# The end of a streaming top-10 kernel: its last three tiles scheduled by hand, with finer exponentials, split gathers, and one batch's rows on the scalar engine

## Chip, cores and metric

One core of one Trainium2 chip. The metric is the device time of one execution in microseconds (us); lower is better. The kernel before took 683.44 us (median of 3 runs, 682.90 to 683.74).

The rounds of the experiments ran on three chips, always with the kernel before beside them, so runs of different rounds are compared by their ratio to it. A time is about 1.8 us more than the span of the profile of the same run.

## The reference

```python
def setup_inputs():
    return {"x": np.random.randn(8192, 8192).astype(np.float32), "k": 10}

def reference(x, k):
    indices = np.argpartition(x, -k, axis=1)[:, -k:]
    values = np.take_along_axis(x, indices, axis=1)
    sorted_idx = np.argsort(-values, axis=1)
    return np.take_along_axis(indices, sorted_idx, axis=1)
```

For each of 8192 rows: the positions of the ten largest of 8192 numbers, largest first. x is 268 MB, and every byte of it must be read once.

## The kernel before

The rows go through in 64 tiles of 128 rows (4 MB). A row is folded over several partitions, and in each tile this happens:

1. *load*: four or eight transfers on the SyncE queue bring in the tile; four x buffers.
2. *weigh*: ACT computes exp(36 (x - 4.7)) into a bf16 tile `e`, and PE adds up groups of columns of it with one-hot matrices. A group that holds one of the top ten has a large sum.
3. *choose*: DVE finds the 12 largest sums (two searches of eight, with a replacement between) and makes indices of them.
4. *gather*: GpSimd copies the candidates of the chosen groups.
5. *spread* and *extract*: a multiplication by a mask, half on DVE and half on GpSimd, and 12 fp32 matmuls (24 passes on PE) bring each row's candidates together.
6. *rank*, three tiles later: DVE takes the top ten of 96 or 192 candidates.
7. *finish*, once per batch of eight tiles or fewer: positions are turned into column numbers (slot, low, two products over a one-hot tile, a sum, the value), spread out as `rows`, moved across partitions by PE ("moves"), copied and written out.

The last three tiles, 61, 62 and 63, use a thin layout (16 partitions to a row, 2 KB pieces). The last batches are of 7, 6 and 3 tiles. At the very end a check counts that all went well, and otherwise a slow loop does the work again. The parts that the change touches:

```python
PAD = 208                       # a spacer tile of 208 floats, allocated ahead of the x buffers
...
    epool = ctx.enter_context(tc.tile_pool(name="e", bufs=3))
...
    nsums = 2 * ntiles + 3      # one checked sum per activation; the size of eall and good
...
    def weigh(t):
        ...
        parts = [S // 4, S // 4, S // 4, S // 8, S // 8] if t == last else [S // 2, S // 2]
        for h, n in enumerate(parts):
            e = epool.tile([P, N // 2], bf16, tag="e", name="e")
            nc.scalar.activation(out=e[:, 0:n * W], in_=xts[t][...], func=ACTF.Exp, ...)
            ...                                   # the sums of this part, on PE
...
        for t in range(last):                     # every engine keeps this order
            interleave(choose_steps(t), rank_steps(t - LAG) if t >= LAG else [])
            if t >= 1:
                spread(t - 1)
            gather(t)
            weigh(t + 1)
            if 1 <= t < last - 2:
                extract(t - 1)
            ...                                   # some finish steps of an earlier batch
        extract(last - 3)
        extract(last - 2)
        run(choose_steps(last))
        spread(last - 1)
        gather(last)
        extract(last - 1)
        ...
        run(rank_steps(last - 3))
        run(rank_steps(last - 2))
        steps = finish_steps(batch_of[last - 3])  # the batch of six
        run(steps[:2])
        spread(last, G)
        run(steps[2:7])                           # ends with its rows, on DVE
        extract(last)
        run(steps[7:-2])                          # its six moves
        run(rank_steps(last - 1))
        run(rank_steps(last))
        ...
        final = finish_steps(batch_of[last])
```

## Time and profile before

| before | us |
|---|---|
| time, median of 3 runs | 683.44 |
| span of the trace | 679.8 |
| last byte of x lands | 651.40 |
| DVE's first search in tile 62's sums | 647.00 |
| DVE's first search in the last tile's sums | 653.96 |
| last ranking ends | 672.88 |

The prediction below shows the page's slices, the windows of the tail and the tail's timeline, and reads them. Of the timeline of the kernel before, the columns are start, duration, engine, line, operation, output and inputs, and in brackets how long the engine had been idle and what ended that.

```profile
647.00 0.70 DVE L189 MAX8 wall<-s 128x8 f32<-128x512 f32 x1 [4.73 <-PE s L169]
675.33 0.62 PE L281 MATMUL fo<-rows,send 128*48 128x80 f32 x6 [1.11 <-DVE rows L301]
```

DVE was idle for 4.73 us before the sums of tile 62 came, and for 1.61 us before those of the last tile. The first is room for other work of DVE. The second is slack on the path: tile 62's sums could come 1.61 us later before the last search moved. PE had slack too, for it waited 1.91 us for ACT before tile 62's sums.

### The profile page before, as it was taken

The page shows a single profiled execution, that of the slowest core. Times are in us where ns is not written, and L with a number is a line of the kernel's source. Part 1 is how long each engine was busy: PE and PEld are TensorE (multiplying, and loading weights), DVE is VectorE, ACT ScalarE, POOL GpSimd, SP SyncE. Part 2 cuts the span into 40 slices and gives each one's busy share as a digit, 9 for nine tenths or more (in the row PEclk, how much of TensorE's full clock was granted, in tenths as well). Part 3 has the DMA queues.
Part 4 walks back from the last instruction along what each step waited for, and adds up shares of the span by engine and source line. Part 5 has one row for each costly group of instructions (what it writes and reads, how often), then busy time and mean ns, then how long its engine had stood idle before and what let it go on. Part 6 is the DMA issues. An engine that isn't in the chain of part 4 may idle for free.

```text
span 679.8 us, 7988 instructions
## 1 busy us (share of the span) xinstructions
PE 549.6 (81%) x2690; PEld 339.5 (50%) x2690; DVE 555.5 (82%) x1335; ACT 488.7 (72%) x264; POOL 178.9 (26%) x134
## 2 busy tenths in 40 slices
PE   1577777888887889887987898898888789887887
PEld 0144544554544565553753555655454355454566
DVE  2577878699779978789796998879977889879687
ACT  4777777777777777777777777777777777777740
POOL 0113133313322322313322313322332231331330
PEclk9887887687878768597686768767788768778786
DMA  9999999999999999999999999999999999999910
GB/s 351 420 421 420 422 418 419 421 419 421 420 420 420 421 419 420 421 419 421 420 421 419 421 419 422 418 420 421 419 421 419 421 419 419 420 420 392 385 39 7
DMA packets 73696, 269.77 MB, mean 397 GB/s; under 512 B 4382, under 2 KB 5046, under 8 KB 73654
## 3 DMA queue, kind: packets, MB, share of 16 engines
q1 hardware_dynamic: 72960, 268.54, 96.8%
q10 hardware_dynamic: 694, 0.71, 0.3%
q8 instruction: 21, 0.34, 0.2%
q14 instruction: 21, 0.17, 0.1%
HBM read 268.58 MB, written 0.66 MB: 396 GB/s over the span
## 4 chain that ended last, share of the span: by engine, by line
DMA 62%; PE 10%; DVE 8%; SPq 6%; ACT 5%; issue 4%; POOL 3%; ACTq 0%; DVEq 0%
DMA xt<-in_x_dram 62%; PE s L169 8%; SPq L101 6%; ACT e L162 5%; POOL cand L203 3%; PE g L233 2%; DVE wall L189 2%; DVE m L190 1%; DVE masked L221 1%; DVE cidb L194 0%; DVE cidb L192 0%; DVE wall L193 0%; DVE rows L301 0%; DVE g L246 0%; DVE pick L298 0%
## 5 line engine op out<-in xcount | busy, mean ns | idle before, releaser
L162 ACT ACTIVATE e<-xt,bias 128x4096 bf16<-128x4096 f32 (+2 forms) x131 | 475.5, 3630 | 155.4 <-DMA xt<-in_x_dram 143.2
L169 PE MATMUL s<-e,group 128*128 128x512 bf16 x1024 | 337.5, 491 | 123.7 <-ACT e L162 123.4
L169 PEld LDWEIGHTS <-group 128*128 128x128 bf16 x1024 | 121.7, 122 | 316.3 <-issue 259.4
L233 PEld LDWEIGHTS g<-cpack,masked 128*128 128x128 f32 x1536 | 206.4, 214 | 16.5 <-issue 5.4
L233 PE MATMUL g<-cpack,masked 128*128 128x8 f32 (+1 forms) x1536 | 199.1, 269 | 1.7 <-DVE masked L221 1.7
L203 POOL INDIRECT_COPY cand<-xt,idx 128x192 f32 x64 | 64.9, 1014 | 478.8 <-DMA xt<-in_x_dram 181.8
L189 DVE MAX8 wall<-s 128x8 f32<-128x1024 f32 (+1 forms) x64 | 77.2, 1206 | 116.2 <-PE s L169 116.1
L221 POOL TENSOR_TENSOR masked<-cand,cpack 128x768 f32<-128x768 f32 x63 | 113.1, 1795 | 5.3
L192 DVE FIND_INDEX8 cidb<-wall,s 128x8 uint16<-128x1024 f32 (+1 forms) x64 | 76.6, 1197 | 0.0
L194 DVE FIND_INDEX8 cidb<-wall,m 128x8 uint16<-128x1024 f32 (+1 forms) x64 | 76.3, 1193 | 0.0
L190 DVE MATCH_REPLACE8 m<-wall,s 128x1024 f32<-128x1024 f32 (+1 forms) x64 | 76.0, 1188 | 0.0
L193 DVE MAX8 wall<-m 128x8 f32<-128x1024 f32 (+1 forms) x64 | 75.6, 1181 | 0.0
L221 DVE TENSOR_TENSOR masked<-cand,cpack 128x768 f32<-128x768 f32 x64 | 61.4, 960 | 0.9 <-POOL cand L203 0.9
L281 PE MATMUL fo<-rows,send 128*64 128x160 f32 (+3 forms) x128 | 27.9, 369 | 1.1 <-DVE rows L301 1.1
L162 ACT ACTIVATION_READ_ACCUMULATOR e<-xt,bias 128x1 f32 x131 | 24.4, 186 | 0.0
L281 PEld LDWEIGHTS fo<-rows,send 128*64 128x64 f32 (+2 forms) x128 | 18.3, 159 | 3.5 <-DVE rows L301 1.6
L248 DVE FIND_INDEX8 posb<-t8a,g 128x8 uint16<-128x96 f32 (+1 forms) x64 | 16.6, 260 | 0.0
L250 DVE FIND_INDEX8 posb<-t8b,g 128x8 uint16<-128x96 f32 (+1 forms) x64 | 16.4, 255 | 0.0
L245 DVE MAX8 t8a<-g 128x8 f32<-128x96 f32 (+1 forms) x64 | 16.1, 252 | 0.0
L246 DVE MATCH_REPLACE8 g<-t8a,g 128x96 f32<-128x96 f32 (+1 forms) x64 | 16.1, 251 | 0.0
L249 DVE MAX8 t8b<-g 128x8 f32<-128x96 f32 (+1 forms) x64 | 15.8, 246 | 0.0
L362 ACT ACTIVATE e<-tall,bias 128x64 f32<-128x64 f32 x1 | 0.3, 347 | 19.6 <-DVE tall L251 19.6
(37 smaller groups left out, 105.7 us busy)
## 6 DMA issues: line engine op xcount, KB each, us to landing
xt<-in_x_dram SPq DMA_DIRECT2D x248, 1024.0 KB, 16.3
xt<-in_x_dram SPq DMA_DIRECT2D x16, 512.0 KB, 9.4
out_dram<-opack ACTq DMA_DIRECT2D x6, 80.0 KB, 5.2
cpack<-topk_cpack ACTq DMA_DIRECT2D x1, 141.0 KB, 3.3
out_dram<-opack ACTq DMA_DIRECT2D x1, 70.0 KB
out_dram<-opack SPq DMA_DIRECT2D x1, 60.0 KB, 1.9
out_dram<-opack SPq DMA_DIRECT2D x1, 30.0 KB, 1.5
```

The source lines that it names most:

```text
L101: nc.sync.dma_start(out=dst[:, s:s + n, :], in_=src[:, s:s + n, :])
L162: nc.scalar.activation(out=e[:, 0:n * W], in_=xts[t][:, s0 * W:(s0 + n) * W], func=ACTF.Exp, bias=bias[:, 0:1], scale=BETA, accum_out=eall ...
L169: nc.tensor.matmul(ss[t][:, j:j + BANK], lhsT=lay.group[:, s0 + i, :], rhs=e[:, i * W + j:i * W + j + BANK], start=s0 + i == 0, stop=s0 + ...
L189: lambda: nc.vector.max(out=w16[:, 0:8], in_=m),
L190: lambda: nc.vector.match_replace(out=m2, in_to_replace=w16[:, 0:8], in_values=m, imm_value=-1.0),
L192: lambda: nc.vector.max_index(out=cid[:, 0:8], in_max=w16[:, 0:8], in_values=m),
L193: lambda: nc.vector.max(out=w16[:, 8:16], in_=m2),
L194: lambda: nc.vector.max_index(out=cid[:, 8:16], in_max=w16[:, 8:16], in_values=m2),
L203: nc.gpsimd.add_instruction(mybir.InstIndirectCopy(name=nc.get_next_instruction_name(), ins=[nc.gpsimd.lower_ap(xts[t]), nc.gpsimd.lower_a ...
L221: eng.tensor_tensor(out=masked[t][:, g0:g1], in0=cand[:, g0:g1].unsqueeze(2).to_broadcast(shape), in1=layout(t).own.rearrange("p (c s) -> ...
L233: nc.tensor.matmul(gs[t][:, c * R:(c + 1) * R], lhsT=mk[:, c, :, :].rearrange("p a s -> p (a s)"), rhs=layout(t).place, start=True, stop=True)
L281: nc.tensor.matmul(fo, lhsT=lay.send[:, i, 0:n * S], rhs=rows[:, i].rearrange("p a k -> p (a k)"), start=i == 0, stop=i == n - 1)
```

## The change

Its intent: take work out of the 28 us after the last byte of x. It moves the extraction and ranking of tile 60, and four finish steps of the batch of six, ahead of the last tile's sums; cuts the last tiles' exponentials into smaller parts so that PE can put extractions between the sums; gathers the candidates of the last two tiles in two halves, so that masks start sooner; and gives `rows` of the batch of six to ACT, which is idle by then. The core of the diff (cut; the main loop's order of the index search and the replacement is swapped too):

```diff
-PAD = 208
+PAD = 320
...
+    def parts(t):
+        S = layout(t).S
+        if t < ntiles - TAIL:
+            return [S // 2] * 2
+        return [S // 4] + [S // 8] * 5 + [S // 16] * 2 if t == last else [S // 4] * 4
...
-    nsums = 2 * ntiles + 3
+    first_sum = np.cumsum([0] + [len(parts(t)) for t in range(ntiles)]).tolist()
+    nsums = first_sum[-1]
...
+        early = t >= last - 1
         return [
             lambda: nc.vector.max(out=w16[:, 0:8], in_=m),
+            lambda: nc.vector.max_index(out=cid[:, 0:8], in_max=w16[:, 0:8], in_values=m),
+        ] + ([lambda: index(0, G // 2), lambda: gather(t, 0, G // 2)] if early else []) + [
             lambda: nc.vector.match_replace(out=m2, ...),
-            lambda: nc.vector.max_index(out=cid[:, 0:8], in_max=w16[:, 0:8], in_values=m),
             ...
+        def spread_rows():
+            if b != len(starts) - 2:
+                return nc.vector.tensor_tensor(out=rows, ..., op=ALU.mult)
+            for a in range(A):
+                nc.scalar.activation(out=rows[:, :, a, :], in_=val, func=ACTF.Copy,
+                                     scale=lay.own_a[:, a:a + 1])
...
-        extract(last - 3)
-        extract(last - 2)
-        run(choose_steps(last))
-        ...                                       # the old tail, shown above
+        a, b, c = last - 2, last - 1, last        # tiles 61, 62, 63
+        run(later)
+        wb, wc = weigh_steps(b), weigh_steps(c)
+        run(wb[0:3])
+        extract(a - 1, 0, 6)
+        run(wb[3:4])
+        extract(a - 1, 6, G)
+        run(wc[0:4])
+        run(rank_steps(a - 2))
+        mask(nc.gpsimd, a, G // 2, G)
+        run(choose_steps(b))
+        mask(nc.vector, a, 0, G // 2)
+        extract(a, 0, 2)
+        run(wc[4:5])
+        extract(a, 2, 4)
+        run(wc[5:])
+        extract(a, 4, G)
+        run(rank_steps(a - 1))
+        steps = finish_steps(batch_of[a - 1])
+        run(steps[:4])
+        mask(nc.gpsimd, b, G // 2, G)
+        chosen = choose_steps(c)
+        run(chosen[:4])
+        mask(nc.vector, b, 0, G // 2)
+        run(chosen[4:])
+        extract(b)
+        run(steps[4:7])
+        mask(nc.vector, c, 0, G // 2)
+        extract(c, 0, G // 2)
+        ...
+        run(rank_steps(a))
+        mask(nc.vector, c, G // 2, G)
+        extract(c, G // 2, G)
+        run(steps[7:])
+        run(rank_steps(b))
+        run(rank_steps(c))
```

## The prediction

> **What bounds the kernel now.** I read the page first, from the slices down to the chain, then two stretches of the end in the table of windows, then the timeline of the last 40 us line by line.
>
> ```profile
> span 679.8 us, 7988 instructions
> PE   1577777888887889887987898898888789887887
> DVE  2577878699779978789796998879977889879687
> ACT  4777777777777777777777777777777777777740
> DMA  9999999999999999999999999999999999999910
> GB/s 351 420 421 420 422 418 419 421 419 421 420 420 420 421 419 420 421 419 421 420 421 419 421 419 422 418 420 421 419 421 419 421 419 419 420 420 392 385 39 7
> ...
> DMA 62%; PE 10%; DVE 8%; SPq 6%; ACT 5%; issue 4%; POOL 3%; ACTq 0%; DVEq 0%
> ```
>
> The DMA row stands at 9 in 38 of 40 slices and the rate is flat at 420 GB/s: until about 651 us nothing but the arrival of x sets the time, and PE, DVE and ACT all have idle time. The last two slices are different: DMA and ACT are done, PE and DVE are not. The last three tiles use the thin layout (2 KB rows), and the rate in their slices is 392 and 385. By the landing times in the trace the last 4 MB tile arrives in eight pieces from 642.4 to 651.4 us, 1.29 us apart. So 679.8 - 651.4 = 28 us of tail after the last byte is all that this change can touch; the 651 us before it stay.
>
> ```profile
> core 0: us, PE busy (x) PEld busy (x) DVE busy (x) ACT busy (x) POOL busy (x), PEclk, DMA share, GB/s
> 653.90:672.90 19.00, 19.00 (x105) 18.51 (x104) 17.55 (x56) 0.00 (x0) 3.54 (x3) 0.59 0.00 1
> 672.90:679.80 6.90, 2.13 (x13) 1.17 (x11) 3.31 (x12) 0.35 (x1) 0.00 (x0) 0.75 0.05 15
> ```
>
> The tail has two parts. From the last tile's sum (653.9) to the end of its ranking (672.9), DVE is busy 17.55 of 19.0 us and PE all of it: both are bounds, and a change must relieve both. ACT has nothing to do there. From 672.9 on comes a serial end of 6.9 us (last batch's rows, the move, the check, the branch).
>
> ```profile
> 651.40 0.95 DVE L221 TENSOR_TENSOR masked<-cand,cpack 128x768 f32<-128x768 f32 x1
> 652.05 1.13 ACT L162 ACTIVATE e<-xt,bias 128x1024 bf16<-128x1024 f32 x1
> 653.54 17.21 PEld L233 LDWEIGHTS g<-cpack,masked 128*128 128x128 f32 x96
> 653.96 0.70 DVE L189 MAX8 wall<-s 128x8 f32<-128x512 f32 x1 [1.61 <-PE s L169]
> 658.30 0.94 DVE L221 TENSOR_TENSOR masked<-cand,cpack 128x768 f32<-128x768 f32 x1
> 663.66 1.76 DVE L221 TENSOR_TENSOR masked<-cand,cpack 128x1536 f32<-128x1536 f32 x1 [0.88 <-POOL cand L203]
> 668.03 1.16 DVE L301 TENSOR_TENSOR rows<-val,cpack 128x960 f32<-128x960 f32 x1
> 672.75 0.14 DVE L251 COPY tall<-t8b 128x1 f32<-128x1 f32 x1
> 677.16 0.15 DVE L377 CAST ngood<-gps 1x1 int32<-1x1 f32 x1 [0.37 <-PE gps L375]
> ```
>
> The third line is four extractions (tiles 60 to 63, 24 passes each) in one lump after the last sum, although the masks of tile 60 were ready 18 us earlier. The other lines mark DVE's way through the tail; its only real waits there are 1.61 us on the last sum and 0.88 us on the gather of tile 63.
>
> **What the Trainium skill says.** "TensorE: Matmul & The Clock Gate", Part 1: the array's clock is half until the monitor has seen a busy window of about 3.4 us, and falls back after an idle one. The trace agrees on the two values and the 3.4 us grid, but not on what counts as busy: from 657.5 us the clock is 0.5 for 17 us although the extractions run back to back. One pass takes 110 ns before and 214 ns after that, so 24 passes are 2.65 or 5.1 us. I expect half clock again once the 512-wide sums end.
>
> "ScalarE: Activation LUTs", What ACT_TABLE_LOAD costs: an activation with a [128,1] pointer operand takes about 280 ns + 0.833 ns per element, overlapping its neighbour by 93 ns. The trace agrees: 2048 columns take 1.98 us, and starts are 1.99 apart. Table sets: copy is in every set, so the new copies should need no second table load; no run here shows that yet.
>
> "SBUF — State Buffer", Who interferes with whom: a DVE instruction with two SBUF inputs contends with a GpSimd one that reads SBUF. GpSimd's mask takes 1.80 us beside a busy DVE and 1.54 late in the tail, so this is a few tenths, off the path.
>
> **The change part by part.** Durations are start-to-start distances in the timeline of before: choosing a thin tile 4.34 us (653.96 to 658.30), ranking 1.34 (96 columns) or 1.86 (192), half a mask 0.94, slot and low 0.27, the two products over the one-hot tile 0.93 and 0.57, their sum and the value 0.93 and 0.26, rows 1.07.
>
> *Exponentials.* ACT takes 1.99, 1.13 and, extrapolated, 0.68 us for 2048, 1024 and 512 columns. Tile 61 and 62 go from two to four activations, the last from five (2048 x3, 1024 x2) to eight (2048, 1024 x5, 512 x2). That is about 0.25 us more per extra one, some 1.8 us in all, against pieces that can start earlier. But only three e buffers remain, so each activation now waits for the sums three parts back. In tile 61 the fourth waits: PE is in the moves of an earlier batch until 632.85, so I put its start at about 634 in place of 630.75. In the last tile the fourth and eighth wait behind extractions in PE's order. Following ACT and PE part by part I get the last sum at 653.4 if no buffer binds and 654.5 if they do, against 653.96. No gain from this part; its use is to have sums of tile 62 out near 646.1 (before: 647.0).
>
> *Extractions between sums.* Tile 60's extraction and a third of tile 61's go before the last sum. After it PE has 16 + 24 + 24 passes in place of 96. At half clock the 32 removed are 6.9 us, but PE is only one of two bounds.
>
> *DVE between last sum and last ranking.* Before: 18.91 us. Moved ahead of the last sum: tile 60's ranking (1.34) and four steps of the six-tile batch (0.27 + 0.93 + 0.57 = 1.77). Moved to ACT: rows (1.07). The wait for the gather (0.88) goes, since half the candidates are gathered early and other work lies in the way. Added: one more index instruction, 0.3, and a split mask, 0.15. 18.91 - 1.34 - 1.77 - 1.07 - 0.88 + 0.45 = 14.3 us. Moved work must fit before the last sum: from tile 62's sum at 646.1, choose 4.2 (with the extra index), mask 0.94, rank 1.34, four steps 1.77 make 654.3. So DVE arrives just as the last sum does; I take 654.3 as the start.
>
> *Does PE follow?* The last half mask of tile 63 ends 14.3 - 1.86 - 1.86 = 10.6 us after the start, at 664.9; its 12 passes at half clock take 2.6, plus 0.2 to be seen, 667.7; DVE has ranked tile 62 by 666.7. So DVE waits 0.9 us. Last ranking ends 654.3 + 14.3 + 0.9 = 669.5 (before 672.87).
>
> *ACT's rows.* 16 copies of 60 columns. An estimate from the skill's figures: 280 + 50 - 93 = 237 ns each, 3.8 us, from about 661 to 665, under the extractions. Then 12 move passes on PE after the last extraction, 3.44 us at half clock (670.79 in before), end near 671, when the last batch needs PE at about 672. Just hidden.
>
> *The end.* The last batch's steps are the same: 6.93 us. 669.5 + 6.93 = 676.4, that is 3.4 us under 679.8. Median: 683.44 - 3.4 = 680.0. Splitting the last loads and the wider check cost nothing on this path. I choose 679.7, a little lower, because the buffer waits are the term I took most harshly.
>
> **The rivals.** (1) PE stays the bound: everything after 657 at half clock, moves and extractions queue, and the last batch's move waits for the other batch's twelve passes. For it: half clock for 17 us in before. Against: 32 passes fewer. Gain 1.5 us or less: 681.9 or more. (2) ACT becomes the bound at the end of the stream, through the added fixed cost and the three buffers; the last sum comes at 655.5 or later, and everything after shifts by that. For it: in before ACT runs without a gap from 641.2 to 653.2. Against: pieces arrive 1.29 us apart and 1024 columns need 1.13. It would make about 681.5. (3) All waits vanish: the sum at 653.4, PE at full clock, the rankings back to back: 653.4 + 14.3 + 6.9 = 674.6, a time of 678.2. (4) The shifted buffer addresses (x moves by 512 bytes) or the swapped order of the index search and the replacement in the main loop change the stream itself. The DMA rate is flat at 420 GB/s whatever DVE does, so I expect nothing; were it 1%, that would be 7 us either way.
>
> **Range and chances.** The sum gives 680.0; rivals 1 to 3 span 678.2 to 682. Range 677.2 to 682.0. 2% is 13.7 us, half of the tail, more than removing all of DVE's moved work could give; so faster by 2% has 1%, slower 1% (only through rival 4), within 2% 98%.
>
> **What would show it.** Right: the chain is DMA until 651, the last sum near 654.3, DVE without a long gap from 646 to 669, the last ranking near 669.5, 16 short activations under the extractions, a last part of 6.9 us. Wrong: a gap over 1.5 us ahead of the last ranking with PE named (rival 1); ACT activations late behind PE releases and the last sum past 655 (rival 2); another DMA rate in the middle slices (rival 4); or a second table load.

## The result, and the profile after

The changed kernel took 682.18 us (median of four runs: 680.32, 681.59, 682.78, 683.04), beside 683.28 for the kernel before in the same rounds. The ratio is 0.998, with a 95% interval of 0.9957 to 1.0003: the same time. A ratio here is the mean time of one kernel's fast runs over the mean of the other's in the same rounds, so it is not quite the ratio of the two medians. The class was predicted; the time was not. 682.18 lies 0.2 us above the range, and 2.5 above the predicted time.

The stations of the tail, each read from the timelines:

| us | predicted | before | after |
|---|---|---|---|
| DVE's first search in tile 62's sums | 646.1 | 647.00 | 649.40 |
| DVE's first search in the last tile's sums | 654.3 | 653.96 | 658.11 |
| from there to the end of the last ranking | 15.2 | 18.92 | 15.41 |
| from there to the end of the span | 6.93 | 6.94 | 7.44 |
| span | 676.4 | 679.8 | 681.0 |

So the tail after the last sums did become 3.5 us shorter, nearly as predicted. But the last sums are searched 4.15 us later, although the last byte of x lands at the same time (651.40 before, 651.45 after). The gain was given away ahead of the stretch that was tuned.

From the page of the changed kernel, the rate of each slice, and the shares of the chain that ended last:

```profile
GB/s 360 420 422 420 420 420 418 421 419 421 419 421 420 419 420 420 421 418 422 420 421 419 421 419 421 419 420 421 419 422 419 420 419 421 418 419 382 370 29 7
...
PE 5%; DVE 1%; issue 0%; ACT 0%; DVEq 0%
```

The middle slices still move 420 GB/s, so the stream itself is as before. The chain has changed: before, it came back to the DMA of x for 62% of the span; now no transfer of x is in it at all. It breaks off before it gets to one. What is in it, in order of time (start, duration, what):

```profile
642.96 4.29 PE s L183 x12
647.25 1.24 PE g L264 x12
648.49 0.89 PE s L183 x4
```

PE's own queue leads to DVE's search at 649.40: twelve sums of tile 62, then the first twelve passes of the extraction of tile 60 (L264), then the last four sums of tile 62. The timeline shows the rest of the story:

```profile
637.21 2.00 ACT L176 ACTIVATE e<-xt,bias 128x2048 bf16<-128x2048 f32 x1 [6.90 <-PE s L183]
649.40 0.70 DVE L217 MAX8 wall<-s 128x8 f32<-128x512 f32 x1 [2.28 <-PE s L183]
650.94 0.86 DVE L209 TENSOR_SCALAR idx<-cidb,cpack 128x6 uint16<-128x6 uint16 x1
658.11 0.70 DVE L217 MAX8 wall<-s 128x8 f32<-128x512 f32 x1
664.36 3.88 ACT L319 ACTIVATE rows<-val,cpack 128x60 f32<-128x60 f32 x16 [7.18 <-DVE val L348]
671.58 0.37 DVE L277 MAX8 t8a<-g 128x8 f32<-128x192 f32 x1 [1.67 <-PE g L264]
676.04 1.03 PE L330 MATMUL fo<-rows,send 128*48 128x80 f32 x6 [1.14 <-DVE rows L314]
```

The line at 658.11 has no bracket: DVE did not wait for the last sums. It ran from 649.40 to 658.11 without a gap, through its choice in tile 62, a mask, the ranking of tile 60 and four finish steps, and only then could it turn to the last tile. The search in the last tile is no longer tied to the arrival of x. It is tied to tile 62's sums, 8.71 us ahead of it. The first line is an exponential of tile 61, the last of its four parts. It waited 6.90 us for an `e` buffer, which PE had not yet read.

The same in windows: first the approach to tile 62's sums, before and then after, and then after's tail. The columns are named in the first line of the second fence.

```profile
631.90:649.40 17.50, 13.92 (x66) 7.23 (x65) 11.22 (x39) 14.64 (x11) 6.87 (x5) 0.85 0.89 339
```

```profile
core 0: us, PE busy (x) PEld busy (x) DVE busy (x) ACT busy (x) POOL busy (x), PEclk, DMA share, GB/s
631.90:649.40 17.50, 17.00 (x86) 10.81 (x86) 10.24 (x38) 12.19 (x13) 3.31 (x4) 0.78 0.90 339
658.10:673.50 15.40, 15.40 (x72) 14.92 (x72) 13.31 (x44) 3.88 (x16) 3.03 (x3) 0.50 0.00 1
```

In this window of 17.5 us, which ends where after's tile 62 is searched, PE went from 13.9 us of work to 17.0: it is full. A part of the rise is the lower clock (0.78 in place of 0.85). The work that was moved out of the tail sits in PE's queue in front of the sums that the tail now starts from.

The theories that I then had:

- **A, the buffer wait.** Rival 2 of the prediction: the 6.90 us wait of ACT for an `e` buffer delays every part after it. Without the wait the sums come as predicted.
- **B, DVE's chain behind PE's queue.** The end is tile 62's first search plus 8.7 plus 15.3 plus 7.3 us, whatever ACT does, and tile 62's search is set by the work in PE's queue ahead of it, and by the clock at which PE does it.
- **C, the stream.** Other buffer addresses or the swapped order in the main loop cost something.

### The profile page after: what moved, and what is told of

The parts are those of the page before. It is cut to its first block, busy times and chain, and to the rows that moved or that the text cites. A ratio compares the mean times of both kernels' runs of the same rounds, so it can differ in the third digit from the quotient of the medians.

```text
span 681.0 us, 8025 instructions
## 1 busy us (share of the span) xinstructions
PE 552.1 (81%) x2690; PEld 342.3 (50%) x2690; DVE 556.2 (82%) x1336; ACT 494.9 (73%) x295; POOL 181.0 (27%) x136
## 5 line engine op out<-in xcount | busy, mean ns | idle before, releaser
L264 PEld LDWEIGHTS g<-cpack,masked 128*128 128x128 f32 x1536 | 209.4, 216 | 19.0 <-issue 8.6
L264 PE MATMUL g<-cpack,masked 128*128 128x8 f32 (+1 forms) x1536 | 201.0, 270 | 2.6 <-DVE masked L247 2.6
L230 POOL INDIRECT_COPY cand<-xt,idx 128x192 f32 (+1 forms) x66 | 66.7, 1010 | 479.5 <-DMA xt<-in_x_dram 196.3
L209 DVE TENSOR_SCALAR idx<-cidb,cpack 128x12 uint16<-128x12 uint16 (+1 forms) x66 | 14.7, 223 | 0.2
```

The lines of the kernel that those rows point to most:

```text
L230: nc.gpsimd.add_instruction(mybir.InstIndirectCopy(name=nc.get_next_instruction_name(), ins=[nc.gpsimd.lower_ap(xts[t]), nc.gpsimd.lower_a ...
L264: nc.tensor.matmul(gs[t][:, c * R:(c + 1) * R], lhsT=masked[t][:, c, :, :].rearrange("p a s -> p (a s)"), rhs=layout(t).place, start=True, ...
```

## The experiments

There were 18 runs, of 16 kernels. The gather could not be run again in experiments. A stand-in takes its place: two short GpSimd additions on the same operands. Their result is wrong, 99% of the indices differ, and the final test is set so that the slow loop is not taken. So every edit below is compared with a control that has the stand-in as well, and none of these versions is a working kernel.

```diff
-        nc.gpsimd.add_instruction(mybir.InstIndirectCopy(...))     # xts[t] at idxs[t] -> cands[t]
+        spots = ...                                                # fixed places of xts[t]
+        for src in (spots, cands[t]):
+            nc.gpsimd.tensor_tensor(out=cands[t], in0=src, in1=idxs[t] as fp16, op=ALU.add)
...
-    with tc.If(passed < checks):
+    with tc.If(passed < 1):
```

All medians, with the ratio to the kernel before in the same rounds; that kernel's median in the five groups of rounds was 683.25, 683.28, 683.64, 683.51 and 683.38:

| run | what it is | median us (lowest to highest, runs) | ratio [95%] |
|---|---|---|---|
| c_before | before, stand-in | 683.39 (682.60–684.08, 5) | 1.0002 [0.9989, 1.0015] |
| c_after | after, stand-in | 680.67 (680.11–682.08, 5) | 0.9964 [0.9951, 0.9976] |
| e_oldparts | c_after, old parts; buffers shifted unawares | 698.79 (698.66–699.81, 5) | 1.0232 [1.0219, 1.0246] |
| e_ring | c_after, `e` as a ring of six quarters | 680.88 (678.17–681.84, 6) | 0.9965 [0.9953, 0.9978] |
| e_ring_sp | e_ring, one output transfer on SP | 678.91 (678.38–681.43, 6) | 0.9943 [0.9929, 0.9957] |
| e_oldparts2 | c_after, old parts, buffers aligned | 682.06 (680.76–684.13, 5) | 0.9981 [0.9969, 0.9994] |
| e_pad208 | c_after with PAD 208 | 696.30 (695.79–696.80, 2) | 1.0192 [1.0174, 1.0210] |
| e_ring_again | e_ring once more | 682.06 (1) | – |
| e_late60 | c_after, extraction of 60 behind tile 62's sums | 679.71 (677.93–681.46, 6) | 0.9941 [0.9925, 0.9956] |
| e_moves | c_after, seven moves behind tile 62's sums | 680.55 (679.27–682.61, 6) | 0.9962 [0.9947, 0.9977] |
| e_mask61 | e_ring_sp, half a mask ahead of tile 62's search | 678.42 (677.38–680.18, 6) | 0.9929 [0.9916, 0.9941] |
| e_best | ring, SP, moves, late60, mask61 | 680.45 (678.81–681.10, 5) | 0.9946 [0.9933, 0.9958] |
| e_rowsdve | c_after, rows back on DVE | 680.86 (680.45–681.08, 5) | 0.9967 [0.9954, 0.9980] |
| e_warm | e_mask61, 12 unread wide matmuls | 681.04 (680.28–683.27, 6) | 0.9975 [0.9959, 0.9990] |
| e_warm_dense | e_mask61, 24 unread wide matmuls | 684.45 (682.97–685.26, 6) | 1.0019 [1.0005, 1.0032] |
| e_best2 | e_mask61, both masks and extraction of 61 early | 677.94 (676.99–683.83, 6) | 0.9945 [0.9918, 0.9973] |
| e_best3 | e_best2 with late60 | 679.89 (677.98–680.46, 6) | 0.9942 [0.9928, 0.9956] |
| e_best2_again | e_best2 once more | 679.03 (677.75–684.21, 6) | 0.9945 [0.9918, 0.9973] |

And the stations of the traces that the argument uses (us; "half clock" is the share of the stretch from 615 to 640 us in which PE's granted clock was 0.5, worked out from its mean; the last column is the mean granted clock from 626.9 to 636 us):

| trace | tile 62's search | last tile's search | to last ranking's end | to the end | span | half clock | clock 627–636 |
|---|---|---|---|---|---|---|---|
| after | 649.40 | 658.11 | 15.41 | 7.44 | 681.0 | 0.68 | 0.50 |
| c_before | 648.32 | 654.27 | 20.39 | 6.95 | 681.6 | 0.28 | 0.62 |
| c_after | 648.85 | 657.68 | 15.14 | 7.45 | 680.3 | 0.40 | 0.62 |
| e_ring | 645.39 | 654.22 | 15.14 | 7.03 | 676.4 | 0.30 | 0.81 |
| e_ring_again | 649.24 | 658.08 | 15.14 | 7.03 | 680.2 | 0.68 | 0.50 |
| e_ring_sp | 646.28 | 655.12 | 15.15 | 7.43 | 677.7 | 0.18 | 0.81 |
| e_oldparts2 | 651.39 | 660.23 | 14.95 | 7.18 | 682.4 | 0.43 | 0.51 |
| e_late60 | 647.27 | 656.16 | 15.15 | 7.44 | 678.7 | 0.22 | 0.81 |
| e_moves | 645.20 | 654.87 | 15.14 | 7.43 | 677.5 | 0.41 | 0.62 |
| e_mask61 | 646.36 | 654.57 | 15.13 | 7.02 | 676.7 | 0.18 | 0.81 |
| e_rowsdve | 646.79 | 655.64 | 15.83 | 7.37 | 678.8 | 0.48 | 0.80 |
| e_best2 | 645.35 | 654.42 | 13.77 | 7.02 | 675.2 | 0.18 | 0.81 |
| e_best2_again | 648.38 | 657.46 | 13.77 | 7.02 | 678.3 | 0.41 | 0.52 |

### The controls

> Control. The kernel before, with the gather on GpSimd replaced by two short GpSimd additions on the same operands (the gather itself is not to be run again), so its output is wrong. If the stand-in is fair, the time is within 0.3% of the kernel before (682 to 685 us), the last sum is used near 654 us and the last ranking ends near 673.

> Control. The changed kernel with the same stand-in. If fair: 0.2% under the kernel before (681 to 683.5 us). In the trace the fourth activation of tile 61 waits for PE (6.9 us in the first trace), the last sum is used near 657 to 658 us, later than before. The clock theory (the late sums were one unlucky phase of the clock) expects that this stall is absent or under 3 us here.

Measured: the stand-in leaves the kernel before where it was (1.0002), and the changed one at 0.9964, a little under the 681 to 683.5 us expected; the runs overlap with those of the real one (680.11 to 682.08 beside 680.32 to 683.04), and so do the intervals. Of the controls' traces the first search lines of the timelines, of c_before and of c_after:

```profile
648.32 0.70 DVE L189 MAX8 wall<-s 128x8 f32<-128x512 f32 x1 [4.62 <-PE s L169]
654.27 0.70 DVE L189 MAX8 wall<-s 128x8 f32<-128x512 f32 x1 [0.60 <-PE s L169]
```

```profile
636.67 2.00 ACT L176 ACTIVATE e<-xt,bias 128x2048 bf16<-128x2048 f32 x1 [5.92 <-PE s L183]
657.68 0.69 DVE L217 MAX8 wall<-s 128x8 f32<-128x512 f32 x1
```

The pattern is that of the real kernels: ACT waits 5.92 us for a buffer, and DVE has no wait ahead of the last search. In c_before tile 62's sums came 1.32 us later than in the trace of before (648.32 against 647.00), and the last search only 0.31 us later: the wait before it shrank from 1.61 to 0.60 instead. That is the slack at work. One station of c_before is not that of before: the last ranking ends 20.39 us after the last search in place of 18.92, with 0.70 and 0.85 us of waiting for PE, at a mean clock of 0.55 in place of 0.59. How much of this comes from the stand-in is not shown.

### The buffer wait (theory A)

e_ring keeps the bytes of `e` and hands them out in quarters of a tile, so that six quarter parts can be in flight where there were three buffers:

```diff
-    epool = ctx.enter_context(tc.tile_pool(name="e", bufs=3))
+    ering = consts.tile([P, 6, N // 4], bf16, name="ering")
...
-            e = epool.tile([P, N // 2], bf16, tag="e", name="e")
+            need = max(1, n * W * 4 // N)          # quarters of a tile; a half takes two
+            q = slot_no[0] % 6
+            slot_no[0] += need
+            e = ering[:, q:q + need, :].rearrange("p q j -> p (q j)")
```

> The changed kernel with the same SBUF bytes for e cut into a ring of six quarters: a half tile takes two, all smaller parts take one, so a quarter no longer occupies a half's place. Buffer theory: no ACT wait on PE in tile 61, last sum at 653.5 to 655, 3 to 4 us under the changed control. PE theory: ACT waits elsewhere, the last sum moves by less than 1 us and so does the time.

The trace showed the predicted schedule to a few tenths: tile 62's sums at 645.39, the last search at 654.22, a span of 676.4. It looked like a full proof of theory A. But the profiled run was the fastest of six (678.17), and the median, 680.88, did not move from c_after's 680.67. So the same kernel was looked at again:

> The ring once more, for a second trace: the first profiled run (span 676.4) was the fastest of six (678.2 to 681.8 us). Clock theory (the fast one was lucky with the PE clock between 615 and 640 us: half clock for 30% of it): a run near 681 shows more half clock there and a last sum at 656 or later. If it shows a last sum at 654 and still 681, the time is lost after the last sum.

Timelines of e_ring and of e_ring_again:

```profile
645.39 0.70 DVE L221 MAX8 wall<-s 128x8 f32<-128x512 f32 x1 [3.11 <-PE s L187]
654.22 0.69 DVE L221 MAX8 wall<-s 128x8 f32<-128x512 f32 x1
```

```profile
637.58 2.00 ACT L180 ACTIVATE ering<-xt,bias 128x2048 bf16<-128x2048 f32 x1 [4.17 <-DVE opack L328]
649.24 0.70 DVE L221 MAX8 wall<-s 128x8 f32<-128x512 f32 x1 [2.28 <-PE s L187]
```

And one window of each, with the same columns as above (the clock is the third number from the right):

```profile
615.00:640.00 25.00, 22.05 (x126) 14.54 (x124) 24.16 (x62) 20.04 (x17) 10.78 (x8) 0.85 1.03 390
```

```profile
615.00:640.00 25.00, 22.46 (x99) 15.03 (x98) 20.42 (x44) 18.29 (x15) 11.31 (x8) 0.66 1.02 388
```

One kernel, two executions, 3.85 us apart at tile 62's search, and 3.8 us apart in the span: everything after that search has the same length, 31.0 us. PE was busy for the same 22 us of these 25, but at a mean clock of 0.85 it finished 126 matmuls, and at 0.66 only 99. This is theory B's picture: PE's queue sets the start, the rest is a fixed chain. In the slower of the two ACT's wait has another reason: its queue holds the transfer of the 7-tile batch's output (DVE opack), which has to wait for the moves.

e_ring_sp takes that transfer off ACT's queue, and issues it on SyncE's after the last loads:

```diff
-        queue = nc.sync if b >= len(starts) - 2 else nc.scalar
+        queue = nc.sync if b >= len(starts) - 3 else nc.scalar
...
-            todo = {last - 5: 6, last - 4: TB, last - 3: TB}.get(t, 3)
+            todo = {last - 5: 6, last - 4: TB, last - 3: 1}.get(t, 3)
```

> The ring of six quarters, and the output DMA of the seven-tile batch issued by SP after the last loads in place of ACT, where it stood between the activations of tile 61 and 62 and made ACT's queue wait for DVE's copy (2.7 us in the ring's trace). Buffer theory, extended (ACT loses its lead in tile 61 by two waits, the e buffers and this issue): ACT never waits for anything but loads from tile 60 on, the last sum comes at 653.5 to 654.5, and all runs lie near 678 (0.7 to 0.9% under the kernel before). PE theory (PE, slowed by spells of half clock, is late itself, so freeing ACT does nothing): the median stays at 680 to 681 as with the ring alone, and in the trace the sums wait for PE while finished e parts lie ready.

Measured 678.91, ratio 0.9943, about 1.5 us better than c_after. The intervals still touch (e_ring's begins at 0.9953, this one ends at 0.9957). The time is near what the extended buffer theory expected (678) and not the 680 to 681 of the PE theory. But the sign of the PE theory is in the trace: tile 62's last part was ready at 643.10, and PE came to it at 645.22. Doing away with the buffer wait alone gains nothing; with it, a queue that does not hold ACT up is worth some 0.2%. Its trace has half clock for only 18% of the stretch, so the trace alone does not say how much is due to the edit.

The other way to undo the wait is to go back to the old, larger parts:

```diff
-        return [S // 4] + [S // 8] * 5 + [S // 16] * 2 if t == last else [S // 4] * 4
+        return [S // 4] * 3 + [S // 8] * 2 if t == last else [S // 2] * 2
```

with the last tile's loads in eight pieces again, and the tail's order kept as near as the larger parts allow.

> The changed kernel with the activations and loads of the last three tiles cut as in the kernel before (halves; the last 3 quarters and 2 eighths), all else as changed. Buffer theory (three e buffers now hold three quarters of a tile in place of one and a half tiles, so ACT stalls behind PE): the stall of tile 61 goes, the last sum comes at 654 to 655, and the time falls by 2 to 4 us against the changed control. PE theory (after the last sum PE at half clock sets the end, and the sums were late because PE was late): within 0.7 us of the changed control.

This one failed as a test of the parts, with 698.79 us: the number of checked sums fell from 138 to 131, two constant tiles shrank with it, and the x buffers landed at an address where the whole stream is slower (next section). Mended with `PAD = 336`:

> As the run with the parts of the kernel before, but with 16 more words of padding so that the x buffers start at a multiple of 512 bytes again; in the first try they started 448 bytes past one, and the whole stream ran at 409 in place of 420 GB/s. If that was the cause: 420 GB/s, and a time near 680. Buffer theory: last sum at 654 to 655 and 678.5 to 680; PE theory: within 0.7 us of the changed control (680.7).

Measured 682.06, slower than c_after by some 0.17% (1.2 us; the intervals overlap, so this is likely rather than certain), although the long buffer wait in tile 61 is gone. Both expectations were missed. In its trace tile 62's sums came at 651.39, but this is the slowest of the five runs. The finer parts, with their wait, are at least no worse than the old ones without it. **Theory A falls** as the cause of the whole miss: both ways of undoing the wait alone left the time where it was, or worse.

That does not make the wait free, for it delays ACT's parts of tile 62 too. In c_after ACT finished the last of them at 646.62, and PE, busy with its queue, came to it at 647.79. So two paths to tile 62's sums end within 1.2 us of each other, and whoever shortens one alone soon waits for the other.

### The padding (theory C)

```diff
-PAD = 320
+PAD = 208
```

> The changed control with the padding left at 208 words as before the change, which puts the x buffers 64 bytes past a multiple of 512. If the alignment of the loads' targets rules the stream: about 409 GB/s and 697 to 699 us, 2.3% slower than the kernel before; if the first slow run had another cause: 680 to 682.

Measured 696.30, ratio 1.0192. Here is the line of rates on its page:

```profile
GB/s 352 409 409 410 408 409 408 410 408 409 409 409 409 409 409 408 410 408 409 409 409 410 409 408 410 409 410 409 409 408 409 410 407 409 409 409 372 375 105 7
```

409 GB/s in place of 420, all through the stream. Worked out from the allocations, the x buffers start on a partition at byte 94208 in before and 94720 in after, both multiples of 512. With 208 in the changed kernel they start at 94272, which is 64 past such a multiple; in e_oldparts at 94656, 448 past one; and both of these streams run at 409. So the edit of the padding, which looks idle, is needed: the change adds seven checked sums, their tiles grow, and the larger pad brings the buffers back to such a multiple. Without it the change would have cost 2%. The prediction read this edit as harmless, which is true of the pair as it stands, for a reason that it did not see. In theory C nothing is left: after's stream runs at 420 GB/s and its last byte lands at the same time.

### What stands in PE's queue ahead of tile 62's sums (theory B)

Theory B says: take work from ahead of these sums in PE's order and the end moves, even with ACT's wait left alone. e_late60:

```diff
-        run(wb[0:3])
-        extract(a - 1, 0, 6)
-        run(wb[3:4])
-        extract(a - 1, 6, G)
+        run(wb[0:4])
+        extract(a - 1)
```

> The changed control with one edit in PE's order: the first half of tile 60's extraction goes behind the last quarter of tile 62's sums instead of in front of it. Chain theory (from tile 62's sum on, DVE is one unbroken chain: 8.8 us to the last tile's first search, 15.2 to the last ranking, 7.0 to 7.5 to the end, seen alike in six traces; so the time is set by when PE delivers tile 62's sum): that sum comes 1.2 to 2.6 us earlier, and so does the end, unless ACT (last activation at 656 in the control, because of its stall in tile 61) binds: then 0 to 1 us. Buffer theory alone (ACT's stall sets the last sum): no change over 0.4 us.

Measured 679.71, ratio 0.9941 against 0.9964: with twelve passes put behind the sums instead of ahead of them the time is lower by 0.23%, or 1.6 us (the intervals overlap by 0.0005 at their edges). ACT's wait was still 4.5 us. The trace does not bear out that the edit made all of this. Tile 62's search came 1.58 us earlier than in c_after, but PE had started tile 61's sums, which lie ahead of the edit, 1.12 us earlier already (634.43 against 635.55). About 0.46 us is left for the edit, and then PE waited 0.64 us for ACT: the other path bound. On top of e_best2 the same edit gained nothing (e_best3, below).

e_moves puts the seven moves of the 7-tile batch, about 4 us of PE, behind tile 62's sums too (and their copy and transfer behind that, on SP):

```diff
-            todo = {last - 5: 6, last - 4: TB, last - 3: TB}.get(t, 3)
+            todo = {last - 5: 6, last - 4: 1, last - 3: 0, last - 2: 0}.get(t, 3)
...
-        run(later)
         wb, wc = weigh_steps(b), weigh_steps(c)
         ...
         extract(a - 1, 6, G)
+        run(later[:-2])                            # the seven moves
...
+        run(later[-2:])                            # their copy and transfer
         run(steps[:4])
```

> The changed control, three e buffers as they were, but the seven moves of the seven-tile batch stand on PE behind tile 62's sums and tile 60's extraction in place of in front of tile 61's sums (their copy and output DMA follow later, the DMA from SP). Chain theory with PE's order as the cause: tile 61's sums start 3.4 to 4 us earlier, ACT's stall in tile 61 (5.9 us) falls under 2.5, tile 62's sum comes at 645 to 646.5, time 677.5 to 679 (2 us or more under the control). Buffer theory: the stall stays above 4 us and the time at 680 to 681.

Measured 680.55: a miss. Its trace has tile 62's sums early, at 645.20, as expected, and ACT's wait down to 2.9 us (under 2.5 expected). But the last search came 9.67 us later in place of 8.8. The copy went into DVE's chain (0.31 us), and at its end DVE waited 0.76 us for PE, which now had the moves in front of the last sums. The work was not taken away. It was put in front of the next thing that someone waits for. e_best, which joins all edits so far and the next one, met the same fate:

> All together: ring, moves and extraction of tile 60 behind tile 62's sums, output DMA on SP, tile 61's mask early. Chain theory: tile 62's sum at 643.5 to 644.5 (its last activation ends near 643), last search at 652.5 to 653.5, where ACT's and the loads' end bind again, end 22.3 later: 675 to 676.5 in the trace, 676.5 to 678 by the clock outside. If PE's half clock sets the end whatever the order: 678 to 680.

Measured 680.45, ratio 0.9946, no better than e_mask61 alone (0.9929; the intervals overlap); its DVE waited 2.37 us for PE before the last search.

One comparison of these traces is the clearest. Ahead of tile 61's sums PE has tile 58's extraction (24 passes) and the seven moves (14 passes). The change did not touch this work. Here it is on PE's timelines, of before and of after:

```profile
626.82 2.74 PE L233 MATMUL g<-cpack,masked 128*128 128x8 f32 x24
629.49 3.36 PE L281 MATMUL fo<-rows,send 128*56 128x160 f32 x14
```

```profile
626.93 5.12 PE L264 MATMUL g<-cpack,masked 128*128 128x8 f32 x24
631.98 3.98 PE L330 MATMUL fo<-rows,send 128*56 128x160 f32 x14
```

It began at the same time, and tile 61's sums followed at 632.78 in before and at 635.89 in after: 3 us later, at a mean granted clock of 0.50 in place of 0.81 (from 626.9 to 636 us). The last column of the table of stations gives this clock for each trace. Leave out c_before, which has the old order, and e_moves, which takes the moves out of this stretch. Then the versions with a clock of 0.80 or 0.81 search tile 62 at 645.35 to 647.27, and those with 0.50 to 0.62 at 648.38 to 651.39. Two kernels stand in both groups: e_ring (645.39 and 649.24) and e_best2 (645.35 and 648.38). And e_rowsdve, which up to there has the same instructions as c_after, has 646.79 where c_after has 648.85. The clock theory in c_after's expectation had been dropped because ACT's wait came again; but in that execution too the clock was low (0.62). No experiment set the clock, and what makes it differ between executions is not shown.

### DVE's chain

If DVE's chain from tile 62's search sets the last search, shortening it must help. e_mask61 starts from e_ring_sp and does half a mask of tile 61 ahead of that search, where DVE waits anyway:

```diff
+        mask(nc.vector, a, 0, G // 2)
         run(choose_steps(b))
-        mask(nc.vector, a, 0, G // 2)
```

> The ring with the output DMA on SP, and tile 61's half mask on DVE moved ahead of the wait for tile 62's sum, into DVE's idle time there. Chain theory: the distance from tile 62's first search to the last tile's falls from 8.8 to 7.9 us, and the time by 0.9 us against the ring with SP (678.9), to about 678. If the last sum is set by PE or ACT and not by DVE's chain: no change of the last sum and of the time.

Measured 678.42, ratio 0.9929, against 0.9943 for e_ring_sp: 1.0 us by the ratios, whose intervals overlap. The trace shows the effect itself: the distance between the two searches fell from 8.84 to 8.21 us, less than the 0.9 us expected. A line of its PE timeline:

```profile
657.34 10.39 PE L267 MATMUL g<-cpack,masked 128*128 128x16 f32 x48 [2.26 <-DVE masked L250]
```

This line is what sets the 15.1 us after the last search. The 48 passes of tiles 62 and 63 run as one lump for 10.39 us, 216 ns each, at half clock, and they start only when DVE has masked tile 62, some 2.8 us after the last search. DVE waits for them before its last ranking (1.67 us in the trace of after). So in this stretch PE is the bound, and it is one at half clock.

e_best2 acts on this: the mask of tile 62 too goes ahead of the last search, and the extraction of tile 61 is put between the last sums.

```diff
-        run(wc[0:4])
+        run(wc[0:2])
...
-        extract(a, 0, 2)
-        run(wc[4:5])
-        extract(a, 2, 4)
-        run(wc[5:])
-        extract(a, 4, G)
+        extract(a, 0, 3)
+        run(wc[2:3])
+        extract(a, 3, 6)
+        ...                                        # and so on: 6:8, 8:10, 10:G between parts 3 to 6
+        run(wc[6:])
...
-        run(chosen[:4])
-        mask(nc.vector, b, 0, G // 2)
+        mask(nc.vector, b, 0, G // 2)
+        run(chosen[:4])
         run(chosen[4:])
```

> The best kernel so far, with all of tile 61's extraction between the last sums and tile 62's half mask ahead of the last tile's search, so that PE can start tile 62's extraction at the last sum. PE theory of the end: last sum to last ranking falls from 15.1 to 13.4 (then DVE's own sum binds), the last sum comes 0.95 later by the mask: 0.8 us faster, about 677.6. If DVE binds there already: 0 to 0.3 us change.

From its PE timeline:

```profile
654.65 3.65 PE L267 MATMUL g<-cpack,masked 128*128 128x16 f32 x24 [0.72 <-DVE masked L250]
660.71 5.51 PE L267 MATMUL g<-cpack,masked 128*128 128x16 f32 x24 [2.40 <-DVE masked L250]
```

Tile 62's 24 passes now start right at the last search, partly at full clock (3.65 us), and the stretch to the last ranking falls from 15.13 to 13.77 us. The mask that moved now lies ahead of the last search, which comes 9.07 us after tile 62's in place of 8.21; so of the 1.36 us gained 0.5 us remain. Five of six runs took 676.99 to 679.41 us, and one 683.83. The repeat, and then e_late60's edit on top of it:

> The same kernel again beside it: one of its six runs was at 683.8, the other five at 677.0 to 679.4. If that one was chance, the median stays within 0.7 us of 677.9 and no run is above 681; if it is a second state of this version, one run in five or so is near 683 again.

> The fastest version so far (ring, output DMA on SP, early masks of tile 61 and 62, tile 61's extraction between the last sums; 677.9) with tile 60's extraction behind tile 62's sums, which alone was worth 1.0 us on the changed control. Chain theory: tile 62's sum 1 us earlier, all else alike, about 677. If the last loads and ACT bind the last sum there (last activation ends at 653 in the trace), 0 to 0.4 us.

Again five runs took 677.75 to 680.04 us and one 684.21, at a mean clock (0.779) no lower than the others'. So that one run in six seems to belong to this version; I did not find its cause. Because of it the mean gains nothing on e_mask61. e_best3 did not show it in six runs, which is too few to rule it out, and is no better at 679.89, where 677 to 677.9 was expected: in its trace DVE waited 1.94 us for PE before the last search, since tile 60's whole extraction now stood ahead of the last sums. In its six runs the clock can be seen at work: the two runs with a mean granted clock of 0.787 and 0.797 took 678.13 and 677.98 us, the four with 0.761 to 0.772 took 679.86 to 680.46. This is a correlation, and it is not there in every version (in e_warm there is none).

### Rows on ACT

```diff
-            if b != len(starts) - 2:
+            if True:                               # DVE makes the rows of every batch
                 return nc.vector.tensor_tensor(out=rows, ...)
```

> The changed control with one part undone: the six-tile batch's rows are spread by one DVE product again in place of 16 activations on ACT. The prediction's step (DVE binds after the last sum): 1.07 us slower than the changed control (680.7), about 681.7, with the last sum to last ranking at 16.2 us. PE theory for this stretch (48 passes of extraction at half clock, 10.4 us, follow tile 62's mask and end just ahead of the last ranking; 15.1 us in every trace): 0 to 0.5 us slower.

Measured 680.86 against 680.67 (ratios 0.9967 and 0.9964): not told apart. In the trace the stretch to the last ranking is 15.83 us against 15.14. So ACT's rows are worth 0.7 us there and not DVE's 1.07, since DVE would otherwise only have waited for PE.

### Can the clock be held up?

After the 512-wide sums end, PE is busy without a pause and still gets half clock. If the narrow passes do not count as work, wide ones should. e_warm adds an unread 512-wide bf16 matmul after every second extraction matmul of tiles 62 and 63, e_warm_dense after every one:

```diff
             nc.tensor.matmul(gs[t][...], lhsT=masked[t][...], rhs=layout(t).place, ...)
+            if t >= last - 1 and c % every == every - 1:       # every = 2, or 1
+                nc.tensor.matmul(warm[:, 0:BANK], lhsT=thin.group[:, 0, :],
+                                 rhs=thin.group.rearrange("p s j -> p (s j)")[:, 0:BANK], ...)
```

> The best kernel so far (ring, output DMA on SP, early mask of tile 61; 678.4) with a 512-wide bf16 matmul that nobody reads after every second matmul of the last two tiles' extractions: 12 in all, 2.6 us at full clock. If the clock falls because extractions of 16 columns do not count as work and these do: full clock through the extractions, 48 passes in 5.3 + 2.6 = 7.9 in place of 10.4 us, PE no longer ahead of the last ranking, 1 to 2 us faster. If one in four passes is too little, half clock stays and 12 x 0.43 = 5 us are added: slower by 4 to 5 us.

> As before with twice as many unread matmuls, 24. If that holds the full clock: 5.3 + 5.2 = 10.5 us for the extractions, as long as at half clock, so the same time within 0.7 us, but the granted clock after the last sum above 0.9 in place of 0.6. If half clock stays: slower by about 9 us.

Both lost: 681.04 and 684.45, against 678.42 without (in other rounds; by the ratios some 3 and 6 us, less than the 4 to 5 and 9 expected for half clock). A window of e_warm_dense:

```profile
core 0: us, PE busy (x) PEld busy (x) DVE busy (x) ACT busy (x) POOL busy (x), PEclk, DMA share, GB/s
657.00:670.00 13.00, 13.00 (x59) 11.25 (x60) 8.35 (x28) 3.87 (x16) 0.85 (x3) 0.50 0.01 1
```

PE is busy for all 13.00 us and the clock stays at 0.50. The added matmuls cost their own time and released nothing; the stretch to the last ranking grew from 15.13 to 17.77 and 20.66 us. Their operands are one-hot, so mostly zeros, and I cannot exclude that full operands would do better. What governs the clock here stays open.

## Why the prediction was right or wrong, point by point

**The class** (within 2%, 98%) was right, with the reason given: the change can only touch the 28 us of tail.

**The step that failed** is the start of the tail: "its use is to have sums of tile 62 out near 646.1", and from it "DVE arrives just as the last sum does; I take 654.3 as the start". Measured were 649.40 and 658.11. Term by term, the trace is 4.6 us above the predicted 676.4:

| term | predicted | measured | miss |
|---|---|---|---|
| tile 62's sums | 646.1 | 649.40 | 3.3 |
| from there to the last tile's search | 8.2 | 8.71 | 0.5 |
| from there to the last ranking's end | 15.2 | 15.41 | 0.2 |
| from there to the end | 6.93 | 7.44 | 0.5 |

The four runs of the changed kernel spread from 680.32 to 683.04, and the profiled one took 682.78. So in a typical run the first term's miss is somewhat less than 3.3. And 1.8 of the 4.6 us lie in the base: the trace of before, from which the terms come, is of an execution 1.8 us faster than that kernel's median (681.60 against 683.44). The prediction took the saving off the median, so its time was missed by 2.5 us and not by 4.6.

The first term has the size, and two things went wrong in it.

*The clock of PE's queue.* 646.1 was followed through PE with the durations of one fast execution, in which PE's clock ahead of tile 61's sums was 0.81. In the trace of after it was 0.50, the untouched work there took 3 us longer, and tile 62's sums came at 649.40. That queue has no one time: e_ring and e_ring_again are the same kernel and gave 645.39 and 649.24. 646.1 is the time of a good execution; e_rowsdve, with the changed order and a clock of 0.80, came within 0.7 us of it.

*The tie.* I saw that DVE would reach the last sums just as they came. I did not draw the conclusion: a tie means that both ways of getting there have no slack left, and that the start is the *later* of the two. Before, PE waited 1.91 us for ACT ahead of tile 62's sums, and DVE waited 1.61 us for the last sums, so a slower PE reached the end only past these waits. After, 0.51 us of PE's wait is left (at 639.36) and nothing of DVE's, and every microsecond by which tile 62's sums are late goes to the end in full. Ahead of them the change left the seven moves (3.98 us) and added half of an extraction (1.24 us), so that PE was busy 17.0 of 17.5 us.

Shown by runs: the chain of fixed length (31.0 us after tile 62's search in both traces of the ring); that executions of one kernel differ by 3 to 4 us at tile 62's search, together with PE's clock ahead of it; and that a shorter chain of DVE brings the last search nearer (e_mask61). Argued from traces, not set by an experiment: that the clock makes this difference. I had no means to fix the clock. Not shown: that less work in PE's queue makes a typical run faster, since e_late60 has 0.46 us of its own in the trace and e_moves gained nothing.

**The buffers.** "In tile 61 the fourth waits [...] at about 634". It waited, until 637.21, by 3 us more than I thought; at the better clock of e_rowsdve it waited until 634.55, as predicted. To undo that wait alone gains nothing (e_ring), and to go back to large parts gains nothing either (e_oldparts2). Rival 2 named a wait that was there and was not the cause by itself. Its sign, "ACT activations late behind PE releases and the last sum past 655", was met to the letter, and would have led to the wrong verdict without the experiments.

**8.2 us of DVE between the searches** became 8.71. One short instruction in it was stretched, the index instruction at 650.94, 0.86 us in place of 0.23. In e_ring's trace it is another of the kind, at 1.00 us in place of 0.18. In each of the 14 traces looked at, before and the controls among them, one such instruction is stretched so, and it ends 0.01 to 0.04 us after GpSimd's mask does (in after at 651.80 and 651.77). So DVE seems to have been held until GpSimd's mask was done, which cost 0.6 to 1.1 us each time; no run took that mask away to test it. The prediction had a few tenths for such contention, and counted them as off the path. Its own 4.34 us for choosing a tile hold one such instruction (0.84 us at 657.54), and it then used 4.2 with one more index instruction, without working; choosing tile 62 took 4.12 us in e_ring and 4.76 in after.

**The tail of 15.2 us** came out at 15.41 (15.14 in c_after): the size was right, the reason only in part. I had DVE as the bound, with 0.9 us of wait for PE. It waited 1.67 us before the last ranking: PE had 64 passes at half clock to do without a pause, from 657.87 to 671.54. I had followed only the last twelve of them, behind DVE's last mask. Both ways end 13.4 us after the search, and that they agree is luck. Hence rows on ACT gave 0.7 us in the trace (predicted 1.07), and an earlier mask of tile 62 took 1.36 us from this stretch (15.13 to 13.77), of which 0.86 went to the stretch before it.

**The end of 6.93 us** became 7.44. 0.41 of these 0.51 us are the last six moves: 1.03 us at half clock, where the trace of before shows 0.62 at full clock. The prediction expected half clock after the last sums and did not carry it into this term.

**ACT's rows**: 16 copies in 3.88 us, predicted 3.8, with no second table load. Right.

**Two readings.** The masks of tile 60 were not ready 18 us before their extraction but 11.5: DVE's half ends at 642.27, and the mask 18 us before is tile 59's. And GpSimd's 1.54 us late in the tail were measured beside a DVE as busy as elsewhere, so the pair 1.80 and 1.54 does not show contention. No term of the sum rests on either.

**Rival 4** was expected to do nothing and did nothing, but only because the edit keeps the x buffers where the stream is fast.

## What to carry to other kernels

Before you move work out of a tail into the shadow of a stream, write down the idle time of each engine just ahead of the point where the tail begins: that slack is what you are about to spend, and once it is gone the tail starts when the moved work's queue allows, at whatever clock it gets. A tie between two engines in a prediction is not a neutral result; take the later one in a bad execution, and widen the range. And one trace of a kernel whose critical path is on PE can differ from the next by 4 us: repeat it before you believe that it proves an edit. The fastest versions here (e_mask61 at 678.42, e_best2 at 677.94 and 679.03) are 0.5 to 0.7% under the kernel before by the ratios, with the stand-in for the gather; with the real gather they were not run.

## What the Trainium skill lacked or had wrong

- "TensorE: Matmul & The Clock Gate", Part 1, says of the array that "activity releases the throttle", after a busy window of about 3.4 us. In the trace of the changed kernel PE was busy 15.40 of 15.40 us from 658.1 on with a mean clock of 0.50, and with 24 added 512-wide matmuls it was busy 13.00 of 13.00 us, again at 0.50. What counts as activity is missing there.
- No page that I looked at ties the start of a transfer's target in SBUF to its rate. "SBUF — State Buffer", Operand start alignment, is about legality and says that its runs timed nothing; "DMA: Bandwidth & Descriptors", How a descriptor splits into AXI transactions, gives beats for descriptors off a 256-byte boundary, and no rate. Measured with rows of 2 and 4 KB: 420 GB/s with the buffers at a multiple of 512 bytes, 409 GB/s at 64 or 448 bytes past one, 2.3% of this kernel's time (696.30 against 680.67 us). Whether 256 would do was not tried.
